# One ordered stretch of all engines from the mixer to the end, and the up weights of the second feed forward's first pair as events of their own

## The chip, the core and the metric

The kernel runs on one core of a Trainium2 chip. The metric is device time in microseconds (us) of one launch; lower is better. Engines are named as the profile names them: PE (matmuls), PEld (weight loads of PE), DVE, ACT, POOL, and SP, which here only issues DMAs.

## The reference, cut to what matters

One transformer layer on 512 tokens of width 1024, in float32: a feed forward at half weight, a token mixer, a second feed forward at half weight, and a last norm.

```python
x = x + 0.5 * swiglu(rmsnorm(x, ffn1_norm), w_gate1, w_up1, w_down1)
x = x + token_mixer(rmsnorm(x, mix_norm), w_in, w_out, ...)
x = x + 0.5 * swiglu(rmsnorm(x, ffn2_norm), w_gate2, w_up2, w_down2)
return rmsnorm(x, final_norm)

def swiglu(x, w_gate, w_up, w_down):
    return (jax.nn.silu(x @ w_gate) * (x @ w_up)) @ w_down
```

The change lies where the mixer's last product (`w_out`) passes into the second feed forward. That feed forward has 22 tiles of 128 hidden columns, each with a gate and an up product over 1024 inputs (eight steps `k` of 128).

## The kernel before, in words

**Three matmuls for one.** Every float32 operand is split into a high part and a rest (the low part), both in the format that PE multiplies fast. A product is then three matmuls: high by high, high by low, low by high (`mm3`, L143 to L146). The split costs two instructions for each weight block: a cast on ACT that makes the high part, then a subtraction on DVE that makes the low part from the raw block and the high part. So a weight is ready for PE when its DMA has landed, ACT has cast it and DVE has subtracted.

**Places.** Raw weights land in a ring of three buffers (tag `raw`, L130). High and low parts go into a ring of three places in `w_all` (`w_place`, L124 to L127). A new weight waits until PE has read the old one in its place, and a new raw block until DVE has read the old one in its buffer.

**The second feed forward** (`ffn`, L225) has two stages. `turned_front` (L914) makes tiles 0 and 1: it transposes the mixer's result into `xh`/`xl`, runs `first_mm` and `tile_mm` (gate and up of tiles 0 and 1), and prepares combinations of the normed input (`normed_t`, L279, four pairs `p`; tiles `nx`, `th`, `tl`, in the profile `nxb`, `txb`, `ttb`). `gated` (L1010) makes `silu(gate) * up` of a tile and splits it into `ah` and `al`. `pipeline` (L835) then does the up products of the tiles `n1` and `n1 + 1` (`up`, L303; `n1` is 2 here) over 16 steps of 0.68 us, and after them the block units: pairs of tiles by a scheme with seven products instead of eight (`SEVEN`, L46), each product with its own weight. The first unit is `("g", n1)`. Its products are called `a11`, `s3`, `s2`, `a12`, `s1`, `a22`, `s4` here, after the weight that each reads; its first one writes `pwgb` in the profile. The weights `s2` and `s4` are sums that DVE makes (`total`, L396); `s1` and `s3` are summed by a DMA that POOL issues (`weight_sums`, L364).

**What sets the order.** The tile framework lets the order of an engine's instructions be written by hand inside `tc.manual_schedule(engines=...)`. Inside one such stretch an engine takes its instructions as the program issues them. Two stretches that follow each other on the same engine are each kept in order, but a scheduler may weave the second into the end of the first. Before the change, this part of the kernel has three stretches for DVE and ACT: the mixer's (L1761), `turned_front`'s (L1083) and `pipeline`'s (L1085). PE has one stretch over the whole kernel (L90); SP and POOL have one over `turned_front` and `pipeline`. Within `turned_front` and `pipeline` the order comes from planned times: `ev(t, f, ...)` and `at(time, rank, f, ...)` collect calls with a time in us or ns, and the calls are made in the order of these times. The times fix an order and nothing else; on the chip an instruction starts when its engine and its inputs are ready.

**The up weights before the change.** `up_weights(j)` (L313) loads the up weight of tile `j`, casts it and splits it, in one call. For tile `n1` it is called inside `turned_front`, as an event at step 5 of the eight steps of `tile_mm` (L1073). For tile `n1 + 1` it is called first thing in `pipeline`, ahead of the loop over the up products (L877). The raw block is `raw_sub` in the profile, its high and low parts are places of `w`, and the product is `pub`.

**One small instruction** belongs to the stretches too: `wo_tail` (L1874), called from `turned_front`, doubles the gains of the second norm, `V.tensor_scalar_mul(sm[:, 2 * KD:3 * KD], ..., 2.0)`, 128 x 8 elements on DVE.

Of the kernel before, what the change touches and what calls it, by code (L numbers as in the profile page):

```python
# [84 lines left out]
def tile_macaron(ctx: ExitStack, tc, xs, xT, wf, wgu1, wst1, wd1, wdg1, wqk, wvw, wv, wo, wgu2, wst2,  # L85
# [38 lines left out]
    def w_place(shift=0):  # L124
        o = w_used[0] % 3 * 1024 + shift
        w_used[0] += 1
        return w_all[:, o:o + 1024], w_all[:, 3072 + o:4096 + o]  # L127

    def load_w(src, nm, n=1024, shift=0):
        raw = wp.tile([P, 1024], F32, tag="raw", name=f"raw_{nm}")  # L130
        nc.sync.dma_start(raw[:, :n], src)
        return (raw, *w_place(shift))
# [5 lines left out]
    def get_w(src, nm, n=1024, shift=0):  # L138
        raw, h, l = load_w(src, nm, n, shift)
        split_w(raw, h, l, 0, n)  # L140
        return h, l
# [83 lines left out]
    def ffn(wgu, wst, wd, wdg, n0, n1, norm, early, res, nm, hooks, ended, first=None,  # L225
# [77 lines left out]
        def up(j):  # L303

            wh, wl = up_w[j]
            pu = ups[j] = pp.tile([P, S], F32, tag="t", name=f"pu{nm}{j}", bufs=2)
            for k in range(KD):
                o = k // 2 * P + k % 2 * 4 * P
                o = slice(o, o + P)
                mm3(pu[:], wh[:, o], wl[:, o], xh[k][:], xl[k][:], k == 0, k == KD - 1)  # L310
                yield k

        def up_weights(j):  # L313
            up_w[j] = get_w(wst[j - n1][1], f"su{nm}{j}")

        ups, up_w, g = {}, {}, {}
# [31 lines left out]
        def sum_slots(u):  # L348
            if u[0] == "d":
                return GROUP_SUMS[u[2] // 2 % 2]  # L350
            if final is not None:
                if u == units[0]:
                    return TURNED_FIRST
                return GROUP_SUMS[(u[0] == "u") ^ (u[1] in TURNED_PAIRS[1])]
            if u == units[0]:
                return PAIR_SLOTS[0][:2]
            if u[1] == PLAIN + 8:
                return GROUP_SUMS[u[0] == "u"]
            o = 2 if u[0] == "g" else 4
            return PAIR_SLOTS[(u[1] - PLAIN) // 2 % 4][o:o + 2]  # L360
# [155 lines left out]
        def at(time, rank, f, *a):  # L516
            count[0] += 1
            heapq.heappush(events, (time, rank, count[0], f, a))
# [4 lines left out]
        def run(until):  # L523
            while events and events[0][0] <= until:
                _, _, _, f, a = heapq.heappop(events)
                f(*a)
# [308 lines left out]
        def pipeline():  # L835
            seen = {}
            for t, (u, o, p) in enumerate(ops):
                if o[0] == "p":
                    at(starts[t] - 2 * PLAIN_STEP, 1, load, u)
                    at(starts[t] - 3 * STEP, 3, high, t)  # L840
                    at(starts[t] - 2 * STEP, 2.5, low, t)
                elif u[0] == "t":
                    block_events(t)
                elif u[0] == "P":
                    at(starts[t] - (8 if p == 0 else 9) * STEP, 1.5, tiles_load, u, p)
                    at(starts[t] - (3 if p == 0 else 4) * STEP, 4.5, high, t)
                    at(starts[t] - (2 if p == 0 else 3) * STEP, 2.5, low, t)
                else:
                    if t == begin[u]:
                        if u != units[0]:  # L850

                            time, s0 = starts[t] - 14 * STEP, sum_slots(u)
                            if s0 in seen:
                                time = max(time, starts[begin[seen[s0]] + 2])
                            seen[s0] = u
                            if u == ("g", PLAIN + 10) and final is None:


                                time += STEP
                            if u == ("g", TURNED_PAIRS[1][0]) and final is not None:  # L860
                                time += 3 * STEP
                            at(time, 1, weight_sums, u)
                        if final is None:
                            at(starts[t] - 7 * STEP, 1.5, load, u)
                        else:
                            at(starts[t] - 7 * STEP, 1.5, load, u, (0,))
                            at(starts[t] - 5 * STEP, 2.2, load, u, (1,))
                    if o[0] in ("s2", "s4"):
                        at(starts[t] - 5 * STEP, 2, total, t)
                    at(starts[t] - 4 * STEP, 3, high, t)  # L870
                    at(starts[t] - 3 * STEP, 2.5, low, t)
                at(starts[t], 4, product, t)
            if bias is not None:
                at(starts[begin["p", plain]], 5, bias[0])
                for j in range(BIAS_STEPS):
                    at(starts[begin["d", 1, 0] + 2 + j], 5, bias[1], j)
            up_weights(n1 + 1)  # L877
            for i in range(2):
                for k in up(n1 + i):
                    prepared(n1 + i, k)  # L880
                    run((8 * i + k - 15) * 680)
            run(1 << 40)

        def block_events(t):
            u, o, p = ops[t]
            now = starts[t]
            if o[0] in TURNED_AHEAD:
                at(starts[begin[u]] - TURNED_AHEAD[o[0]][u[1]][p] * STEP, 2.2, block_load, u, o[0], p)
            elif o[0] in ("a12", "a22"):
                at(now - 8 * STEP, 1.5, block_load, u, o[0], p)  # L890
            if (u[1], o[0]) == (1, "s4"):
                now = starts[begin[u]] + (TURNED_KEPT[p] + 5) * STEP
            if o[0] in ("s2", "s4"):
                at(now - 5 * STEP, 2, total, t)
            at(now - 4 * STEP, 3, high, t)
            at(now - 3 * STEP, 2.5, low, t)
            if t == begin[u] and u[1] == 1:
                at(now + 2 * STEP, 1, final, "begin", now + 2 * STEP, put, None)
# [10 lines left out]
        def prepared(j, k):  # L909
            if (j, k) in prepare:  # L910
                f, p = prepare[j, k]
                f(p)

        def turned_front():  # L914

            todo = []
            now = [0.0]

            def ev(t, f, *a):
                todo.append((t, len(todo), f, a))  # L920

            def pe(cost, f, *a):
                ev(now[0], f, *a)
                now[0] += cost
# [108 lines left out]
            for hf in range(2):  # L1033
                ev(2.4 + 2.6 * hf, gate_load, hf)
                for c in range(2):
                    t = (7.0, 10.0)[hf] + 0.62 * c
                    ev(t, gate_high, hf, c)
                    ev(t + 0.7, gate_low, hf, c)
            for k in range(KD):
                t = (z[1] + 0.5 + 0.42 * k) if k < 4 else z[2] + 0.5 + 0.42 * (k - 4)  # L1040
# [5 lines left out]
            t0 = now[0]  # L1046
# [10 lines left out]
            for k in range(KD):  # L1057
                t = (t2 if k < 4 else max(t3, t2 + 1.7)) + 0.3 + 0.42 * (k % 4)
# [9 lines left out]
            gated(0, now[0] + 0.1)  # L1068
            for p, t in enumerate((0.2, 4.2, 8.0, 12.0)):
                ev(now[0] + t, normed_t, p)  # L1070
            for k in range(KD):
                if k == 5:
                    ev(now[0], up_weights, n1)  # L1073
                pe(1.36, tile_mm, k)
            gated(1, now[0] + 0.1)
            for _, _, f, a in sorted(todo, key=lambda e: (e[0], e[1])):
# [2 lines left out]
        order = ExitStack()  # L1079
        if final is not None:  # L1080
            prepare = {}
            order.enter_context(tc.manual_schedule(engines={mybir.EngineType.SP, mybir.EngineType.Pool}))
            with tc.manual_schedule(engines={mybir.EngineType.DVE, mybir.EngineType.Activation}):  # L1083
                turned_front()
            with order, tc.manual_schedule(engines={mybir.EngineType.DVE, mybir.EngineType.Activation}):  # L1085
                pipeline()
            return
        for j in range(j0, n1):
# [9 lines left out]
            for hf in range(2):  # L1098
                wh, wl = get_w(wgu[j, hf], f"gu{nm}{j}_{hf}")
                for kk in range(4):  # L1100
                    k = hf * 4 + kk
# [38 lines left out]
    with tc.manual_schedule(engines={mybir.EngineType.DVE, mybir.EngineType.Activation}):  # L1140
        for t in range(4):
            raw = wp.tile([P, 1024], F32, tag="raw", name=f"raw_f{t}")
            h, l = w_place()
            for kk in range(2):
                k = 2 * t + kk
# [74 lines left out]
    n1 = {}  # L1220
# [537 lines left out]
    load(2)  # L1758
    prep(0, True)
    prep(1, True)  # L1760
    with tc.manual_schedule(engines={mybir.EngineType.PE, mybir.EngineType.DVE,  # L1761
                                     mybir.EngineType.Activation}):
        lows = []
        for t in range(max(len(chunks), max(at) + 1)):
            evs = sorted(at.get(t, []), key=lambda e: e[0])
            for r, f, a in evs:
                if r < 10:
                    f(*a)
            if t < len(chunks):
                chunks[t]()  # L1770
            for r, f, a in evs:
                if r >= 10:
                    f(*a)
            for _ in range((t != held["hold"]) + (t - 1 == held["hold"])):
                if lows:
                    lows.pop(0)()
            if later:
                hi_, lo_ = later.pop(0)
                hi_()
                lows.append(lo_)  # L1780
        assert not later
        for f in lows:
            f()
# [277 lines left out]
```

## Time and profile before

| | us |
|---|---|
| median of 3 runs | 922.3 |
| lowest and highest of them | 922.28, 925.2 |
| the profiled execution, its own time | 922.4 |
| its span, first to last instruction | 920.6 |
| granted TensorE clock (share of full) | 0.999 |
| PE busy | 909.9 (99%) |
| DVE busy | 731.8 (79%) |
| ACT busy | 550.5 (60%) |
| POOL busy | 118.5 (13%) |

The profile is one execution. The span runs from the first to the last instruction; the execution's own time is 1.8 us longer. The shares are means over the whole span: DVE's 79% holds stretches that are nearly full and others that are not. A matmul's duration in the timeline is longer than its share of PE's time, because matmuls overlap; the distance from one start to the next is what counts. `L135` and `L136` are the lines of the cast and of the subtraction in the helper `split_w`, `L443` and `L447` those of the block units' weights; a helper's line stands for all who call it, so tiles are named beside lines.

### The profile page before, as it was taken

The numbers are of one execution on the slowest core, as the hardware profiler recorded it, in microseconds if no ns is written. First come the engines' busy times: TensorE is split into PE (matmuls) and PEld (weight loads), VectorE is DVE, ScalarE is ACT, GpSimd is POOL, SyncE is SP. The second block draws the span as 40 slices with busy tenths as digits, with TensorE's granted clock in tenths as the row PEclk, the third lists the DMA queues.
The fourth block names the chain that finished last, engine by engine and source line by source line (L and its number), as shares of the span: only waits on it lengthen the run. The fifth ranks groups of instructions, "written<-read, shape, count | busy, mean of one in ns | idle before, by whom it ended". The sixth has DMA issues, their size and how long they took to land.

```text
span 920.6 us, 16495 instructions
## 1 busy us (share of the span) xinstructions
PE 909.9 (99%) x6014; PEld 829.8 (90%) x6014; DVE 731.8 (79%) x1525; ACT 550.5 (60%) x1155; POOL 118.5 (13%) x157
## 2 busy tenths in 40 slices
PE   9999999999999999999999999999999999999997
PEld 7888999999999998888989778979999889999885
DVE  7797887686888897968876545887887887888786
ACT  7454665345665675656766676656666446666564
POOL 0001100112201100073000000011131012211100
PEclk9999999999999999999999999999999999999999
DMA  7456646578856563457443204375798369787722
GB/s 257 128 146 156 161 116 171 147 171 203 222 137 182 154 173 112 142 154 228 121 116 114 69 30 132 92 180 131 187 236 209 91 181 245 196 190 201 202 70 92
DMA packets 64593, 143.66 MB, mean 156 GB/s; under 512 B 7872, under 2 KB 8384, under 8 KB 64512
## 3 DMA queue, kind: packets, MB, share of 16 engines
q1 hardware_dynamic: 47856, 110.93, 37.3%
q0 software_dynamic: 16656, 31.68, 20.5%
q8 instruction: 47, 0.77, 0.3%
q14 instruction: 34, 0.28, 0.1%
HBM read 135.20 MB, written 4.24 MB: 151 GB/s over the span
## 4 chain that ended last, share of the span: by engine, by line
PE 92%; DVE 4%; DMA 2%; issue 1%; ACT 1%; SPq 0%; DVEq 0%; ACTq 0%
PE pt L145 3%; PE pt L144 3%; PE pt L146 3%; PE pwo L144 2%; PE pwo L146 2%; PE pwo L145 2%; PE pua L146 2%; PE pua L145 2%; PE pua L144 2%; PE pq L144 2%; PE pq L146 1%; PE pq L145 1%; PE pk L144 1%; PE pk L146 1%; PE pk L145 1%; PE pda L146 1%
## 5 line engine op out<-in xcount | busy, mean ns | idle before, releaser
L1508 ACT ACTIVATE pr<-pr,mx 128x128 f32<-128x128 f32 (+3 forms) x64 | 36.1, 565 | 37.4 <-DVE mx L1505 37.3
L1505 DVE CUSTOM_DVE_ANT_0 pr<-sc,strip 128x128 f32<-128x128 f32 (+3 forms) x64 | 30.6, 488 | 19.4 <-PE sc L1503 19.1
L372 POOL DMA_DIRECT2D s1bg<-wst_dram x10 | 8.7, 868 | 271.8 <-DVE fin L1889 160.5
L443 ACT CAST w<-s2a 128x512 fp32r<-128x512 f32 x46 | 28.6, 622 | 15.0 <-DVE s2a L406 12.1
L447 DVE TENSOR_TENSOR w<-s2a,w 128x512 fp32r<-128x512 f32 x46 | 31.6, 686 | 6.5 <-ACT w L443 6.5
L447 DVE TENSOR_TENSOR w<-s2b,w 128x512 fp32r<-128x512 f32 x38 | 26.1, 687 | 9.4 <-ACT w L443 9.4
L1714 POOL DMA_DIRECT2D xn_rows<-xt x32 | 20.6, 655 | 64.1 <-DVE xt L1711 64.1
L443 ACT CAST w<-s2b 128x512 fp32r<-128x512 f32 x38 | 23.6, 620 | 6.3 <-DVE s2b L406 5.5
L144 PE MATMUL pq<-xh,w 128*128 128x512 f32 x64 | 26.7, 417 | 0.0
L144 PE MATMUL pwo<-w,mh 128*128 128x512 f32 x64 | 25.9, 404 | 0.0
L146 PE MATMUL pq<-xh,w 128*128 128x512 f32 x64 | 25.1, 392 | 0.0
L145 PE MATMUL pq<-xl,w 128*128 128x512 f32 x64 | 25.1, 392 | 0.0
L144 PE MATMUL pk<-xh,w 128*128 128x512 f32 x64 | 25.1, 392 | 0.0
L145 PE MATMUL pwo<-w,mh 128*128 128x512 f32 x64 | 25.0, 391 | 0.0
L146 PE MATMUL pk<-xh,w 128*128 128x512 f32 x64 | 25.0, 391 | 0.0
L146 PE MATMUL pwo<-w,ml 128*128 128x512 f32 x64 | 25.0, 391 | 0.0
L145 PE MATMUL pk<-xl,w 128*128 128x512 f32 x64 | 24.9, 390 | 0.0
L1312 DVE TENSOR_TENSOR w<-raw_qk,w 128x512 fp32r<-128x512 f32 x28 | 19.0, 688 | 4.6 <-ACT w L1308 4.5
L145 PE MATMUL pwgb<-xl,w 128*128 128x256 f32 x80 | 22.5, 281 | 0.0
L145 PE MATMUL pxgb<-ttb,w 128*128 128x256 f32 x80 | 22.5, 281 | 0.0
L146 PE MATMUL pwgb<-xh,w 128*128 128x256 f32 x80 | 22.5, 281 | 0.0
L144 PE MATMUL pwgb<-xh,w 128*128 128x256 f32 x80 | 22.5, 281 | 0.0
(712 smaller groups left out, 3946.3 us busy)
## 6 DMA issues: line engine op xcount, KB each, us to landing
raw_qk<-wqk_dram SPq DMA_DIRECT2D x16, 512.0 KB, 3.5
raw0bg<-wst_dram SPq DMA_DIRECT2D x10, 512.0 KB, 5.5
raw0bu<-wst_dram SPq DMA_DIRECT2D x9, 512.0 KB, 6.1
raw_gua<-wgu_dram SPq DMA_DIRECT2D x8, 512.0 KB, 3.4
raw0ag<-wst_dram SPq DMA_DIRECT2D x8, 512.0 KB, 5.1
raw0ad<-wdg_dram SPq DMA_DIRECT2D x8, 512.0 KB, 4.4
strip<-bias_rows SPq DMA_DIRECT2D x16, 256.0 KB, 3.8
raw_wo<-wo_dram SPq DMA_DIRECT2D x8, 512.0 KB, 3.4
```

Source lines behind the costliest of these rows:

```text
L144: T.matmul(po, wh, mh, start=first, stop=False, skip_group_check=on)
L145: T.matmul(po, wh, ml, start=False, stop=False, skip_group_check=on)
L146: T.matmul(po, wl, mh, start=False, stop=last, skip_group_check=on)
L372: nc.gpsimd.dma_start(t[:], b, accum_op=ALU.add)
L443: A.copy(made[t][0], source(t))
L447: V.tensor_tensor(l, source(t), h.bitcast(F32), op=ALU.subtract)
L1312: V.tensor_tensor(l[:, c:c + 512], raw[:, c:c + 512], h[:, c:c + 512].bitcast(F32), op=ALU.subtract)
L1505: V.tensor_tensor_reduce(out=pi, in0=ps[:, :w], in1=st["b"][m][:, w - 1::-1], op0=ALU.add, op1=ALU.min, scale=1.0, scalar=3.0e38, accum_ou ...
L1508: A.activation(pi, pi, AF.Exp, scale=-1.0, bias=st["mx"][:, m, i:i + 1], accum_out=st["ls"][:, m, i:i + 1])
L1714: nc.gpsimd.dma_start(bass.AP(tensor=ap.tensor, offset=ap.offset + m * P + a * NB, ap=[[D, NB], [NB * D, S // NB], [1, NB]]), t[a * NB:(a ...
```

## The change

The diff has three parts.

1. `up_weights(n1)` and `up_weights(n1 + 1)` are taken apart. Load, cast and subtraction become events of `turned_front`: the loads at `t0 + 12` and `t0 + 16`, where `t0` is the planned start of `first_mm`; the casts at 2.6 and 8.4 us after the planned start of `tile_mm`, and the subtractions 1.3 us after each cast. `pipeline` skips its own call.
2. `turned_front` and `pipeline` lose their stretches for DVE and ACT. The one for SP and POOL stays.
3. The mixer's stretch for PE, DVE and ACT is entered on the kernel's exit stack and is left only at the end. So DVE and ACT take all their instructions from the mixer on exactly as the program issues them.

```diff
@@ pipeline
-            up_weights(n1 + 1)
+            if n1 + 1 not in up_w:
+                up_weights(n1 + 1)
@@ turned_front
             for p, t in enumerate((0.2, 4.2, 8.0, 12.0)):
                 ev(now[0] + t, normed_t, p)
+            raw_up = {}
+
+            def up_load(j):
+                raw_up[j], *up_w[j] = load_w(wst[j - n1][1], f"su{nm}{j}")
+
+            def up_high(j):
+                cast(up_w[j][0], raw_up[j][:])
+
+            def up_low(j):
+                rest(up_w[j][1], raw_up[j][:], up_w[j][0])
+
+            for i, t in enumerate((2.6, 8.4)):
+                ev(t0 + 12 + 4 * i, up_load, n1 + i)
+                ev(now[0] + t, up_high, n1 + i)
+                ev(now[0] + t + 1.3, up_low, n1 + i)
             for k in range(KD):
-                if k == 5:
-                    ev(now[0], up_weights, n1)
                 pe(1.36, tile_mm, k)
@@ ffn
-            order.enter_context(tc.manual_schedule(engines={mybir.EngineType.SP, mybir.EngineType.Pool}))
-            with tc.manual_schedule(engines={mybir.EngineType.DVE, mybir.EngineType.Activation}):
+            with tc.manual_schedule(engines={mybir.EngineType.SP, mybir.EngineType.Pool}):
                 turned_front()
-            with order, tc.manual_schedule(engines={mybir.EngineType.DVE, mybir.EngineType.Activation}):
                 pipeline()
@@ the mixer
-    with tc.manual_schedule(engines={mybir.EngineType.PE, mybir.EngineType.DVE,
-                                     mybir.EngineType.Activation}):
+    ordered = ctx.enter_context(ExitStack())
+    ordered.enter_context(tc.manual_schedule(engines={mybir.EngineType.PE, mybir.EngineType.DVE,
+                                                      mybir.EngineType.Activation}))
+    if True:
```

## The prediction

> **What bounds the kernel now.** I read the page of the profile first, then the list of PE's waits, because one row of the page already names the bound.
>
> ```profile
> span 920.6 us, 16495 instructions
> PE 909.9 (99%) x6014; PEld 829.8 (90%) x6014; DVE 731.8 (79%) x1525; ACT 550.5 (60%) x1155; POOL 118.5 (13%) x157
> ```
>
> PE is busy for 99% of the span, so only what makes PE stand still, or lets it run on, can move the end. The view of waits, kept to PE, is short enough to show whole (engine, line, what it waited for: us in total, times, longest):
>
> ```profile
> PE pub L146 <- DVE w L136: 1.4, 1, 1.4
> PE warm L1131 <- POOL ones_d L1125: 1.0, 1, 1.0
> PE pga L1176 <- ACT w L1156: 0.8, 1, 0.8
> PE pub L144 <- ACT w L135: 0.7, 1, 0.7
> PE sc L1503 <- DMA l<-l: 0.2, 1, 0.2
> ```
>
> Two of the five are on `pub`, the product that reads the up weights that the change moves. The windows around it show that this is the only place in the middle of the kernel where PE stops (columns: stretch, length, busy time of PE, PEld, DVE, ACT, POOL, granted clock, DMA share, GB/s):
>
> ```profile
> 593.00:604.10 11.10, 11.10 (x51) 9.01 (x50) 10.13 (x21) 6.09 (x9) 1.19 (x2) 1.00 0.47 149
> 604.10:607.10 3.00, 0.95 (x4) 0.36 (x3) 2.55 (x4) 1.36 (x3) 0.53 (x1) 1.00 0.93 191
> 607.10:617.64 10.54, 10.54 (x46) 8.68 (x47) 9.74 (x22) 6.09 (x13) 1.72 (x2) 1.00 0.66 146
> ```
>
> PE is solid in the first and third stretch and has 0.95 us of work in the 3.00 us between. Note the DVE column too: 10.13 of 11.10 and 9.74 of 10.54. DVE is nearly full on both sides of the gap, so what the gap gives DVE is not free. PE's timeline prices the gap (start, duration, what, idle before it and who ended it):
>
> ```profile
> 603.86 0.39 PE L146 MATMUL pub<-xh,w 128*128 128x512 f32 x1
> 604.95 0.50 PE L144 MATMUL pub<-xh,w 128*128 128x512 f32 x1 [0.70 <-ACT w L135]
> 605.29 0.40 PE L145 MATMUL pub<-xl,w 128*128 128x512 f32 x1
> 607.03 0.50 PE L146 MATMUL pub<-xh,w 128*128 128x512 f32 x1 [1.35 <-DVE w L136]
> 607.38 0.40 PE L144 MATMUL pub<-xh,w 128*128 128x512 f32 x1
> 617.18 0.39 PE L145 MATMUL pub<-xl,w 128*128 128x512 f32 x1
> 617.64 0.28 PE L144 MATMUL pwgb<-xh,w 128*128 128x256 f32 x1
> 617.88 0.28 PE L146 MATMUL pwgb<-xh,w 128*128 128x256 f32 x1
> ```
>
> Undisturbed, 512-wide matmuls start 0.227 us apart and 256-wide ones 0.12. The 48 matmuls of the two `up` products follow the one at 603.86, so the first `pwgb` could start at 603.86 + 49 x 0.227 = 614.97. It starts at 617.64. **The gap and the slow restart behind it cost 2.67 us**, of which about 0.2 is the restart (607.03 to 607.38 is 0.35, not 0.23, and the next few are 0.01 slow).
>
> Why were the weights late? ACT and DVE in the same stretch:
>
> ```profile
> 598.67 1.05 ACT L135 CAST w<-raw_sub 128x1024 fp32r<-128x1024 f32 x1 [0.71 <-PE pub L145]
> 599.62 0.62 ACT L927 CAST ahb<-t1b 128x512 fp32r<-128x512 f32 x1
> 603.86 1.04 ACT L135 CAST w<-raw_sub 128x1024 fp32r<-128x1024 f32 x1
> 598.59 0.69 DVE L1017 TENSOR_TENSOR t1b<-pub,t1b 128x512 f32<-128x512 f32 x1
> 599.75 1.23 DVE L136 TENSOR_TENSOR w<-raw_sub,w 128x1024 fp32r<-128x1024 f32 x1 [0.47 <-ACT w L135]
> 604.55 0.69 DVE L406 TENSOR_TENSOR s2b<-s1bg,raw0bg 128x512 f32<-128x512 f32 x1 [0.66 <-DMA raw0bg<-wst_dram]
> 605.16 0.69 DVE L295 TENSOR_TENSOR ttb<-nxb,txb 128x512 fp32r<-128x512 f32 x1
> 605.76 1.22 DVE L136 TENSOR_TENSOR w<-raw_sub,w 128x1024 fp32r<-128x1024 f32 x1
> ```
>
> There are two up weights. In the order of instructions of the old program the cast at 598.67 waits for PE to free a place: it belongs to the second tile (n1+1, needed last), and the one at 603.86 to the first. The two ordered stretches were woven the wrong way round. DVE also meets a sum of the next unit, which waits 0.66 us for a DMA, ahead of the first tile's low half.
>
> **The change part by part.** The order of instructions of the changed program has the same instructions on every engine, and the same order on PE, SP and POOL. Only DVE and ACT differ, in two places.
>
> *The doubling of the norm's gains* moves from the start of the kernel to the output projection.
>
> ```profile
> 4.62 0.17 DVE L1077 TENSOR_SCALAR x<-x 128x8 f32<-128x8 f32 x1
> ```
>
> At the start PE's only DVE-side neighbour, `pga`, waits for ACT in the list above, not for DVE, so taking 0.17 us off DVE gains nothing. At its new place, between splits of `raw_wo`, the list has no PE wait either. Its bounds are 0.17 us either way; I take 0.
>
> *The up weights and everything behind them.* New order on ACT: `ah` of tile 0, cast n1, two `txb` casts of pair 1, two of pair 2, cast n1+1, `silu` of tile 1, four casts of pair 3, `ah` of tile 1, then the first weights of the block units. DVE follows suit. The sum and splits of the first block unit (`g`, n1), formerly woven in from 604.55 on, now all stand behind `al` of tile 1. The durations, from the groups of this stretch and two timeline rows:
>
> ```profile
> L295 DVE TENSOR_TENSOR ttb<-nxb,txb 128x512 fp32r<-128x512 f32 x6 | 4.1, 688 | 0.2
> L294 ACT CAST txb<-nxb 128x512 fp32r<-128x512 f32 x6 | 3.7, 624 | 5.6 <-DVE nxb L286 4.2 <-DVE nxb L289 1.4
> L299 ACT CAST ttb<-nxb 128x256 fp32r<-128x256 f32 x4 | 1.5, 403 | 0.8 <-DVE nxb L289 0.8
> 601.49 0.42 DVE L285 TENSOR_TENSOR nxb<-nxb 128x256 f32<-128x256 f32 x1
> 601.95 0.42 DVE L286 TENSOR_TENSOR nxb<-nxb,nxb 128x256 f32<-128x256 f32 x1
> ```
>
> A 0.69 us DVE operation lets the next start after 0.60 (605.16 to 605.76); a dependent one starts 0.04 after the end (601.49 to 601.95 is 0.46), and so does a hand-over between engines. From `t1b` at 598.59, which does not move:
> - ACT: `ah` 599.32 to 599.94, cast n1 599.85 to 600.90. DVE: `al` 599.98, low half n1 600.94 to 602.17. PE wants the high half at 604.09 and the low at 604.54. **Both come 2.4 us or more early: the gap at 604 goes**, if the load is there:
>
> ```profile
> 580.85 10.74 SPq L131 DMA_DIRECT2D raw_sub<-wst_dram  x2
> DMA to landing us min/median/max: 3.4/4.0/4.6
> ```
>
> The loads keep their place in SP's queue; the second is issued near 591.3 and lands before 596.
> - DVE, pairs 1 and 2: each takes four `nxb` (4 x 0.46), a wait for the second cast, and two `ttb`, 3.12 us in all: 602.08 to 608.32. Cast n1+1 runs 607.59 to 608.64 on ACT, its low half 608.68 to 609.91 on DVE. PE wants it at 604.09 + 26 x 0.227 = 609.98. That is 0.03 us of room after the hand-over: level.
> - DVE then: `t1b` of tile 1 609.82, four `nxb` from 610.42, four half `ttb` 612.15 to 613.56, `al` 613.56, the sum 614.16, and the low half of `a11`, the first block weight, 614.76 to 615.45. ACT has its high half by 614.05.
> - PE reaches `pwgb` at 614.97 and wants that low half two matmuls later, at 615.21. It comes at 615.49. **A new wait of 0.28 us, PE on DVE.** Behind it every later split gains room (`s3`'s low half 616.05 against 616.9, `s2`'s 616.65 against 618.3), so this wait is the last.
>
> The sum: the third `pwgb` matmul moves from 617.88 to 615.49, a gain of 2.39 us. No restart after so short a stop is in the trace; its cost lies between 0 and the 0.2 after the long one; I take 0.15, nearer to the only row there is. **Gain 2.24 us**, from both sides: 2.67 if DVE is never late, 1.8 if each of eleven hand-overs takes 0.04 more. Nothing behind 618 has a PE wait to absorb or return it. DVE's new standing order delays one load, the raw block of the second unit, which waits for a buffer:
>
> ```profile
> 607.01 0.33 SPq L380 DMA_DIRECT2D raw0bg<-wst_dram  x1
> DMA to landing us min/median/max: 4.9/5.5/9.5
> ```
>
> It follows the second up weight's low half, so 609.95 instead of 607.01; SP's raw and sum loads behind it follow. Even at 9.5 us it lands at 619.5, and PE starts that unit at 625.4: covered. If it were not, each us late would be a us lost.
>
> The profiled execution took 922.4 us with a span of 920.6; 922.4 - 2.2 = 920.2. The median of the runs is 0.1 lower: **920.1 us**, span 918.4.
>
> One rule speaks against packing DVE. A DMA issue of POOL beside it:
>
> ```profile
> 601.30 0.86 POOL L372 DMA_DIRECT2D s1bg<-wst_dram  x1 [16.20 <-DMA s3bg<-wst_dram]
> ```
>
> Both DVE rows at 601.49 and 601.95 lie inside it and last their usual 0.42, so nothing is held up here. The Trainium skill, page "SBUF — State Buffer", section "Who interferes with whom", says that DVE and GpSimd share one port pair as an exclusive lock, for DVE's two-port modes and some two-input operations, and that the later one blocks fully. By that rule the dense DVE stretch would pay for each POOL issue; the two rows above don't bear it out.
>
> **The rivals.**
> - *A: DVE keeps up.* For it: 0.03 and -0.28 us are within the reading error of a chain of twenty steps. The gap goes whole: -2.67, 919.6 us.
> - *B: DVE becomes the bound for longer.* For it: the windows' 10.13 of 11.10. Hand-overs and conflicts cost 1 us more along the chain: gain 1.2, 921.1 us. Against: pitches in the rows repeat to 0.01.
> - *C: POOL's issues hold DVE.* Four fall between 601 and 611, 0.86 us each. If each stops DVE for its length, `a11`'s low half is ready 3.4 us later, at 618.9 instead of 617.88 before: +1.0 and the restart, 923.5 us, slower than before. It decides from 2.4 us of blocking on. Against: 0.42 us inside the POOL row.
> - *D: the change doesn't do what it says.* Excluded for the order, which the changed program shows; left is that something outside the chain moves.
>
> **How the numbers follow.** Forecast 0.68 (919.8 to 920.8); A 0.14; B 0.10; C 0.04; D 0.04, either way. 0.3%, about what a measurement can tell from no change, is 2.8 us: faster means below 919.5, slower above 925.1. The forecast and B lie within. Of A about half falls below 919.5 by scatter, 0.07, and with tails and D 0.12 faster. Slower by that much needs C and more: 0.03. Same 0.85. The range, 919.4 to 921.5, takes in the forecast, A and the better half of B.
>
> **What would show it.** Both PE waits on L135 and L136 at `pub` gone; the low half of n1 done by 602.2; `pwgb` starting near 615.0; one PE wait of about 0.3 us there, on DVE's L447; all else as before. A PE wait on `pub` for the second tile, or on `pwgb` above 0.8 us, is B; DVE operations stretched beside POOL's rows, C; a PE wait for `raw0bg` behind 625 would make the prediction wrong altogether.

## The result, and the profile after

| | us |
|---|---|
| before, median of 12 runs (lowest to highest) | 922.24 (921.72 to 925.2) |
| after, median of 12 runs (lowest to highest) | 920.07 (919.28 to 922.39) |
| ratio after to before | 0.9974, 95% interval 0.9964 to 0.9983 |
| after, the profiled execution and its span | 920.74, 919.0 |

The kernel is 2.2 us faster, 1.6 to 3.3 by the interval; 2.24 was forecast. At 0.26% the result falls just short of the 0.3% that the forecast took as what can be told from no change; the interval, 0.17 to 0.36%, lies on both sides of that bound and wholly on the faster side.

PE's list of waits after the change, whole:

```profile
PE warm L1143 <- POOL ones_d L1137: 1.0, 1, 1.0
PE sc L1515 <- DMA l<-l: 0.4, 1, 0.4
PE pga L1188 <- ACT w L1168: 0.3, 1, 0.3
```

Both rows on `pub` are gone, and no row has come for them. The windows of before, asked of the trace after:

```profile
593.00:604.10 11.10, 11.10 (x55) 9.36 (x54) 9.90 (x20) 5.04 (x7) 1.72 (x2) 1.00 0.45 148
604.10:607.10 3.00, 3.00 (x15) 2.49 (x14) 2.81 (x7) 1.15 (x3) 0.00 (x0) 1.00 1.04 223
607.10:617.64 10.54, 10.54 (x53) 8.75 (x53) 10.06 (x20) 7.58 (x15) 1.74 (x2) 1.00 0.68 155
```

In the middle one PE is now busy for 3.00 us of 3.00 where it was 0.95. DVE, third of the busy columns, is a little fuller than it was, 2.81 for 2.55 and 10.06 for 9.74 in the last two: the stop went, the load of DVE stayed.

This profiled execution cannot be laid over the one of before by its clock time, because it is 0.8 us late long before the change. Its first `pua` and `pga` matmuls show most of it (rows of after, then of before):

```profile
5.62 0.63 PE L1188 MATMUL pua<-eha,w 128*128 128x512 f32 x1
6.05 0.63 PE L1188 MATMUL pga<-eha,w 128*128 128x512 f32 x1
```

```profile
5.62 0.39 PE L1176 MATMUL pua<-eha,w 128*128 128x512 f32 x1
5.86 0.40 PE L1176 MATMUL pga<-eha,w 128*128 128x512 f32 x1
```

The matmuls start 0.43 us apart instead of 0.24, until 6.9 us in the one execution, from 5.6 us on not in the other. In e2 below, matmuls behind a stop start 0.42 to 0.43 us apart at a granted clock of 0.52, so half the clock is the likely reason; it is not shown, since the clock column reads 1.00 for both starts. The change is not the reason: e5, the same kernel, has 0.23 from 5.81 us on, and e1, with the start of before, has 0.43 until 6.20. So times inside the stretch are counted from DVE's product `t1b<-pub` of tile 0, which the change leaves where it was: 598.59 before, 599.38 after.

### The profile page after: what moved, and what is told of

Read it like the earlier page. It is cut to its first block, busy times and chain, and to the rows that moved or that the text cites. A ratio compares the mean times of both kernels' runs of the same rounds, so it can differ in the third digit from the quotient of the medians.

```text
span 919.0 us, 16498 instructions
## 1 busy us (share of the span) xinstructions
PE 910.7 (99%) x6014; PEld 830.8 (90%) x6014; DVE 731.8 (80%) x1525; ACT 549.6 (60%) x1155; POOL 118.2 (13%) x157
## 4 chain that ended last, share of the span: by engine, by line
PE 94%; DVE 3%; DMA 1%; ACT 1%; issue 1%; DVEq 0%; SPq 0%; ACTq 0%
PE pt L146 3%; PE pt L145 3%; PE pt L144 3%; PE pwo L144 2%; PE pwo L145 2%; PE pwo L146 2%; PE pua L144 2%; PE pua L145 2%; PE pua L146 2%; PE pq L144 2%; PE pq L146 1%; PE pq L145 1%; PE pk L144 1%; PE pk L146 1%; PE pk L145 1%; PE pda L146 1%
```

## The experiments

**The theory**, called the order theory in the expectations: two operations for each of two weights stood behind work that waits for late things; put ahead of it, they let PE run on until DVE's chain stops it, by a quarter of a us. **Rivals**: one ordered stretch is enough without the events (stretch theory); the events are enough without the stretch (events theory); only the doubling that left the start counts (start theory); and the forecast's A and B, on how near DVE is to being the bound.

One number of each trace tells them apart better than the median does, since the start and the rest of the run stay out of it: the distance from `t1b` of tile 0 on DVE to the third `pwgb` matmul on PE, the first that needs a block weight's low half. "Chain expected" is worked out from the forecast: 16.90 with its short stop, 16.62 without it, and on top of that the waits or differences that each kernel's expectation gives.

| kernel | distance, us | chain expected | median, us | before, same chip | ratio, 95% interval |
|---|---|---|---|---|---|
| before | 19.29 | | 922.24 | | |
| the change | 16.78 | 16.90 | 920.07 | 922.24 | 0.9974 (0.9964 to 0.9983) |
| e5 the change again | 16.78 | 16.90 | 919.90 | 921.99 | 0.9979 (0.9969 to 0.9989) |
| e1 events only | 19.21 | 19.60 | 923.61 | 922.39 | 1.0013 (1.0004 to 1.0023) |
| e2 stretch only | 21.97 | 20.92 | 925.06 | 922.39 | 1.0034 (1.0021 to 1.0046) |
| e3 two more on DVE | 18.23 | 18.10 | 921.43 | 922.39 | 0.9995 (0.9986 to 1.0004) |
| e4 late split, one tile | 16.62 | 16.62 | 919.61 | 922.39 | 0.9973 (0.9964 to 0.9982) |
| e6 late split, both | 16.63 | 16.62 | 919.92 | 921.99 | 0.9976 (0.9967 to 0.9985) |
| e7 gains first | 16.78 | 16.90 | 919.94 | 921.99 | 0.9977 (0.9968 to 0.9986) |
| e8 first up weight late | 17.54 | 17.42 | 920.68 | 921.99 | 0.9988 (0.9979 to 0.9996) |
| e9 three more on DVE | 18.97 | 18.70 | 922.39 | 921.72 | 1.0009 (0.9993 to 1.0024) |
| e10 four more on DVE | 19.70 | 19.30 | 924.13 | 921.72 | 1.0022 (1.0010 to 1.0034) |

### e1: the events without the stretch

```diff
-            with tc.manual_schedule(engines={mybir.EngineType.SP, mybir.EngineType.Pool}):
+            order.enter_context(tc.manual_schedule(engines={mybir.EngineType.SP, mybir.EngineType.Pool}))
+            with tc.manual_schedule(engines={mybir.EngineType.DVE, mybir.EngineType.Activation}):
                 turned_front()
+            with order, tc.manual_schedule(engines={mybir.EngineType.DVE, mybir.EngineType.Activation}):
                 pipeline()
@@ the mixer
-    ordered = ctx.enter_context(ExitStack())
-    ordered.enter_context(tc.manual_schedule(engines={mybir.EngineType.PE, mybir.EngineType.DVE,
-                                                      mybir.EngineType.Activation}))
-    if True:
+    with tc.manual_schedule(engines={mybir.EngineType.PE, mybir.EngineType.DVE,
+                                     mybir.EngineType.Activation}):
```

> Only the events of the up weights, with the three stretches of before. In its order of instructions the first block unit's sum, cast and split of raw0bg are again woven into the front, now ahead of the second up weight, and the gains are doubled at the start again. Theory (order theory): the gain of the change needs every split that waits for something late to stand behind the up weights; here DVE meets the sum that waits for raw0bg near 603 and ACT the cast of raw0bg near 601.5, both wait until it has landed near 604.5 to 605.3, and the second up weight's high half comes near 610.6 to 611 on the scale of before instead of 608.6. PE waits some 2 us at the second up product, for ACT, and 0.8 more for DVE's low half. Time 922.8 us, 0.6 above before, 2.7 above the change. Rival (events theory): the events alone take the gap away, about 920.1. Rival (start theory): only the doubling that left the start matters; then this one, which has it at the start, stays at 922.2.

923.61 us; the gain is gone and a little more. ACT, DVE and PE in its timeline:

```profile
603.86 0.62 ACT L443 CAST w<-raw0bg 128x512 fp32r<-128x512 f32 x1 [3.18 <-DMA raw0bg<-wst_dram]
603.85 0.69 DVE L406 TENSOR_TENSOR s2b<-s1bg,raw0bg 128x512 f32<-128x512 f32 x1 [1.12 <-DMA raw0bg<-wst_dram]
609.89 1.04 ACT L928 CAST w<-raw_sub 128x1024 fp32r<-128x1024 f32 x1
610.99 0.50 PE L144 MATMUL pub<-xh,w 128*128 128x512 f32 x1 [1.50 <-ACT w L928]
612.25 0.50 PE L146 MATMUL pub<-xh,w 128*128 128x512 f32 x1 [0.53 <-DVE w L931]
```

The first up weight comes early, as with the change. But the block unit's first weight is woven in ahead of the second one, and ACT stands 3.18 us and DVE 1.12 us at the head of their queues for a DMA whose data nobody needs yet. The second cast comes at 609.89, and PE waits where the chain had it wait. Events and start theories had 920.1 and 922.2: the events alone are not enough. In the median it is 0.8 us slower than expected, while its trace is 0.4 quicker; its runs scatter from 921.4 to 926.1. Each run's mean granted clock sorts them: five of the eleven have 0.996 or 0.997 and took 923.4 to 923.9; of the six with 0.998 or 0.999, four took 921.4 to 922.4, the profiled one among them, and two 924.1 and 926.1. So a fall of the clock behind the two stops, as e2 shows one next, is the likelier reason for the 0.8 us. No trace shows such a run, so this is argued, and for the two longest at full clock no reason is known; a late landing of `raw0bg` could be one.

### e2: the stretch without the events

```diff
-            raw_up = {}
...
-            for i, t in enumerate((2.6, 8.4)):
-                ev(t0 + 12 + 4 * i, up_load, n1 + i)
-                ev(now[0] + t, up_high, n1 + i)
-                ev(now[0] + t + 1.3, up_low, n1 + i)
             for k in range(KD):
+                if k == 5:
+                    ev(now[0], up_weights, n1)
                 pe(1.36, tile_mm, k)
```

> Only the one ordered stretch; the up weights are loaded, cast and split in one call each, where they were before. Order theory: the first up weight is cast behind pair 1 of the normed input, the second only behind the last split of tile 1. From the durations of before: the first one's low half is done near 605.3 instead of 604.5 wanted, a wait of 0.8 us; the second one's cast starts when tile 1 is split, near 611.9, so PE waits 2.7 us for it and 0.8 for the low half. pwgb starts 4.0 us later than in the change: 924.1 us, 1.9 above before. Rival (stretch theory): one ordered stretch is what helps, 920.1 to 921. Start theory: the doubling stands late here too, so 920.1.

925.06 us: slower than before, as the order theory had it, and 1 us slower than it had it. PE in the timeline, and the window behind the second stop (the last columns are granted clock, DMA share, GB/s):

```profile
605.27 0.50 PE L146 MATMUL pub<-xh,w 128*128 128x512 f32 x1 [0.52 <-DVE w L136]
610.16 0.39 PE L146 MATMUL pub<-xh,w 128*128 128x512 f32 x1
612.88 0.72 PE L144 MATMUL pub<-xh,w 128*128 128x512 f32 x1 [2.33 <-ACT w L135]
613.39 0.63 PE L145 MATMUL pub<-xl,w 128*128 128x512 f32 x1
```

```profile
612.88:616.00 3.12, 3.00 (x6) 1.92 (x7) 3.12 (x5) 2.12 (x4) 0.96 (x2) 0.52 0.61 93
```

The two stops lie where the chain put them, at 605.3 and 612.9. What it lacked stands in the clock column: 0.52 for 3.1 us behind the stop of 2.33. PE started six matmuls there. About ten would have fitted at full clock, by an estimate from e1's spacings behind its stops, 0.34 us and then 0.23, with the low half ready at 614.09 as here; the slow spacing goes on to 616.43. That is the missing 1.05 us (21.97 against 20.92). All five runs of e2 have a mean clock of 0.996 or 0.997. e9 and e10 ask whether the stop's length did it.

### e3, e9, e10: more work on DVE ahead of the block units

```diff
                 def low_():
-                    rest(al[j][:], gs[j][:], ah[j][:])
+                    for _ in range(1 + 2 * j):
+                        rest(al[j][:], gs[j][:], ah[j][:])
```

> The change, with the last split on DVE ahead of the block units (al of tile 1) made three times instead of once: two more operations of 0.69 us, 0.60 apart, same result. If DVE sets the start of the block units, as the forecast has it, PE waits 1.2 us longer there and nothing gives it back: 921.3 us, 1.2 above the change. Rival A (DVE keeps up and has room): the first 0.6 or more is hidden, at most 0.6 above the change, 920.1 to 920.7.

PE's wait in e3:

```profile
PE pwgb L146 <- DVE w L447: 1.4, 1, 1.4
```

921.43 us, 1.4 above the change; the distance grows by 1.45, where 1.20 was expected. No part of it is hidden: DVE sets the start of the block units, and A's room of 0.6 doesn't exist. That it is more is a matter of size, seen below in e10's row. With 3 and 4 in place of the 2:

> The change with the last split of tile 1 made four times instead of once, same result: PE stands still for about 2.0 us at the third pwgb matmul (1.42 us were measured with two more, and each adds 0.60). Clock theory: the stop of 2.33 us that cost 1.05 us more than its length lost it to the halved clock behind it; a stop of 2.0 us may lie under or over the point from which the clock falls. Under it: 1.8 us above the change, 921.8. Over it: 1.0 to 1.4 more, 923.0, with a granted clock near 0.5 for some 3 us behind the stop. Rival (chance: the clock fell there for a reason of its own): no fall here, 921.8.

> The same made five times: a stop of 2.6 us. Clock theory: longer than 2.33 us, so the clock falls in most executions: 2.4 us for the stop and 1.0 to 1.4 for the clock, 923.4 to 923.8, with a granted clock near 0.5 behind it. Rival (chance): 2.4 us above the change, 922.4, full clock.

The third `pwgb` matmul of e9 and the one after it, and a window of e9:

```profile
617.45 0.39 PE L146 MATMUL pwgb<-xh,w 128*128 128x256 f32 x1 [2.15 <-DVE w L447]
617.67 0.28 PE L144 MATMUL pwgb<-xh,w 128*128 128x256 f32 x1
```

```profile
617.00:620.00 3.00, 2.55 (x21) 2.55 (x22) 3.00 (x6) 2.34 (x5) 0.00 (x0) 1.00 0.01 3
```

The same of e10, with two matmuls a little later:

```profile
614.71 0.28 PE L145 MATMUL pwgb<-xl,w 128*128 128x256 f32 x1
617.88 0.39 PE L146 MATMUL pwgb<-xh,w 128*128 128x256 f32 x1 [2.89 <-DVE w L447]
619.31 0.41 PE L145 MATMUL pzgb<-ttb,w 128*128 128x256 f32 x1
619.52 0.42 PE L146 MATMUL pzgb<-txb,w 128*128 128x256 f32 x1
```

```profile
617.88:619.16 1.28, 1.28 (x11) 1.28 (x11) 1.28 (x3) 1.28 (x4) 0.00 (x0) 1.00 0.00 0
619.16:622.20 3.04, 3.04 (x17) 3.04 (x16) 2.27 (x4) 0.92 (x4) 0.00 (x0) 0.51 0.21 61
```

After e9's idle 2.15 us the clock column stays at 1.00. After e10's 2.89 PE runs 1.3 us at full clock and then drops to 0.51, with 0.21 us between starts where 0.12 is usual, for some 3.3 us until 622.5. So e2's fall was no chance: a stop of this length can bring it. The medians agree: e10 lies 2.4 us above its before, e9 0.7, with an interval that takes in no difference. Both are above what was expected: e9's 922.39 lies between the 921.8 of a kept clock and the 923.0 of a fallen one, e10's 924.13 beyond 923.4 to 923.8. The mean clocks of the runs suggest why for e9: it is 0.996 or 0.997 in three of its ten, the three longest, 923.4 to 926.7. In e10 it is 0.995 to 0.997 in seven of ten. So 2.15 us of idle time may bring the fall too, only less often; this is argued from the means, which do not say where in a run the clock fell. The third and fourth operation cost 0.74 and 0.73 us of distance, not 0.60. DVE's row of e10 says why:

```profile
613.02 3.60 DVE L931 TENSOR_TENSOR alb<-t1b,ahb 128x512 fp32r<-128x512 f32 x5
```

Five operations in 3.60 us are 0.73 from start to start: each writes the tile of the one before, and so starts 0.04 behind its end, as dependent operations do, where independent ones overlap.

### e4 and e6: DVE relieved

e4 moves cast and split of tile 1 behind the first weights of the block units, e6 of both tiles:

```diff
                 ev(t, silu)
                 ev(t + 0.7, up_)
+                if j == 1:
+                    kept_back.extend((high_, low_))
+                    return
                 ev(t + 1.5, high_)
                 ev(t + 2.2, low_)
@@ pipeline
+            for i, f in enumerate(kept_back):
+                at(starts[2 + i], 6, f)
```

> The change, with cast and split of tile 1 (ah, al) moved behind the seven first weights of the block units, where both engines have room; they are needed much later. If DVE is the bound at pwgb by 0.14 to 0.3 us, the short stop there goes and no more: 919.8 to 919.95 us, 0.1 to 0.3 below the change, with no stop at the third pwgb matmul in the trace. If DVE were the bound by much more (rival B), up to 0.6 below. If it isn't the bound, no difference.

> The change, with cast and split of both tiles 0 and 1 moved behind the first weights of the block units. That takes two DVE operations of 0.69 us out of the stretch ahead of pwgb. Order theory: PE is the bound as soon as one of them is out, since moving tile 1's alone took the stop away, so the second brings nothing: 919.6 to 919.9 us, as with one. Rival (DVE still the bound somewhere ahead): 0.6 less than with one, 919.0.

Third `pwgb` matmul and its forerunner in e4, then in e6:

```profile
615.09 0.28 PE L145 MATMUL pwgb<-xl,w 128*128 128x256 f32 x1
615.20 0.28 PE L146 MATMUL pwgb<-xh,w 128*128 128x256 f32 x1
```

```profile
614.36 0.28 PE L145 MATMUL pwgb<-xl,w 128*128 128x256 f32 x1
614.48 0.28 PE L146 MATMUL pwgb<-xh,w 128*128 128x256 f32 x1
```

The spacing is 0.12 in both: the stop is gone with one split moved, and the second brings 0.00 more (16.62, 16.63). PE is the bound from there. In the medians 0.16 us can't be seen; e4's 919.61 and e6's 919.92 don't differ from the change by what these runs can tell.

### e7: the doubling back at the start

```diff
                     V.tensor_scalar_mul(early[0][0][:], x[0], gain(0, 0))
+                    V.tensor_scalar_mul(sm[:, 2 * KD:3 * KD], sm[:, 2 * KD:3 * KD], 2.0)
...
-        ev(-1, V.tensor_scalar_mul, sm[:, 2 * KD:3 * KD], sm[:, 2 * KD:3 * KD], 2.0)
```

> The change, with the doubling of the gains put back to the kernel's start, behind the first high part of x. Order theory: DVE has room there, PE waits for ACT and for the first weights, so no difference: 920.1 us, within 0.3. Rival (start theory): the 0.17 us operation lies on the way to the first low part and comes back whole at the end, 920.3 or more, with PE waiting on DVE in the first ten us.

919.94 us beside 919.90 for the change on the same chip, and PE's list of waits has no row on DVE in the start. The move is worth nothing that shows.

### e8: the first up weight late

```diff
-                ev(now[0] + t, up_high, n1 + i)
-                ev(now[0] + t + 1.3, up_low, n1 + i)
+                if i:
+                    ev(now[0] + t, up_high, n1 + i)
+                    ev(now[0] + t + 1.3, up_low, n1 + i)
             for k in range(KD):
+                if k == 5:
+                    ev(now[0], up_high, n1)
+                    ev(now[0], up_low, n1)
```

> The change, with only the first up weight's cast and split back at step 5 of tile_mm, behind pair 1; the second stays where the change has it. Order theory: the first low half is done near 605.3 on the scale of before instead of the 604.54 wanted; PE waits 0.8 us there. DVE's chain behind it is as long as in the change, so the short stop at pwgb goes in exchange: 0.5 to 0.7 us above the change, 920.6 to 920.8. The second up weight then owns most of the 5 us that the ordered stretch without the events costs. Rival (a stop costs its whole length wherever it lies): 0.9 to 1.0 above, 921.0.

```profile
604.92 0.50 PE L146 MATMUL pub<-xh,w 128*128 128x512 f32 x1 [0.52 <-DVE w L931]
615.65 0.28 PE L145 MATMUL pwgb<-xl,w 128*128 128x256 f32 x1
615.76 0.28 PE L146 MATMUL pwgb<-xh,w 128*128 128x256 f32 x1
```

920.68 us, 0.78 above the change: between the 0.5 to 0.7 of the order theory and the 0.9 to 1.0 of its rival, so the median cannot decide. The distance can. One stop has come, 604.92, and the one at `pwgb` has gone (0.11 between the two). The new stop costs 17.54 - 16.62 = 0.92 us, of which the 0.16 of the old one goes off: 0.76 us, and not its whole length. Of the 5.2 us between e2 and the change the first up weight owns 0.8; the rest is the second one's stop and the clock behind it.

## Why the prediction was right, point by point

Rows of the trace after that carry the chain; ACT, DVE, PE and SP:

```profile
600.62 1.04 ACT L928 CAST w<-raw_sub 128x1024 fp32r<-128x1024 f32 x1
601.70 1.23 DVE L931 TENSOR_TENSOR w<-raw_sub,w 128x1024 fp32r<-128x1024 f32 x1 [0.26 <-ACT w L928]
608.30 1.04 ACT L928 CAST w<-raw_sub 128x1024 fp32r<-128x1024 f32 x1
609.37 1.23 DVE L931 TENSOR_TENSOR w<-raw_sub,w 128x1024 fp32r<-128x1024 f32 x1 [0.25 <-ACT w L928]
615.42 0.68 DVE L447 TENSOR_TENSOR w<-raw0bg,w 128x512 fp32r<-128x512 f32 x1
604.65 0.39 PE L146 MATMUL pub<-xh,w 128*128 128x512 f32 x1
610.77 0.40 PE L146 MATMUL pub<-xh,w 128*128 128x512 f32 x1
615.78 0.28 PE L144 MATMUL pwgb<-xh,w 128*128 128x256 f32 x1
615.90 0.28 PE L145 MATMUL pwgb<-xl,w 128*128 128x256 f32 x1
616.16 0.39 PE L146 MATMUL pwgb<-xh,w 128*128 128x256 f32 x1
616.38 0.28 PE L144 MATMUL pwgb<-xh,w 128*128 128x256 f32 x1
610.62 0.33 SPq L380 DMA_DIRECT2D raw0bg<-wst_dram  x1
```

- **The gap at `pub` goes.** From the last `tile_mm` matmul at 604.65 to the first `pwgb` at 615.78 are 11.13 us for 49 steps, 0.227 each: nothing between them. The first low half is ready at 602.93, 3.55 us after `t1b`; 3.58 was reckoned.
- **The second up weight is level.** Its low half is ready at 610.60 and PE takes it at 610.77: 0.17 us of room, 0.13 after a hand-over of 0.04, where 0.03 was reckoned. A step later in DVE's order, and PE would have stopped here too.
- **A new short wait at `pwgb`.** 615.90 to 616.16 is 0.26, not 0.12: 0.14 us, half of the 0.28 forecast, and too short for a row in the list of waits. The low half of `a11` ends 16.72 us after `t1b`; 16.86 was reckoned. e3 shows that DVE's chain sets this moment, e4 that the stop goes when the chain is shorter.
- **The restart.** 616.16 to 616.38 is 0.22, and 0.12 behind it: 0.10 where 0.15 was taken.
- **The sum.** The distance shrinks by 19.29 - 16.78 = 2.51 us, 2.39 forecast; with the restart 2.41 against 2.24, and 2.2 in the medians. The mechanism came as forecast, but that 920.1 met 920.07 to 0.03 us is luck: the distance was missed by 0.12, and the medians of before alone lie between 921.72 and 922.39.
- **Costed at nothing.** The doubling: e7, 0.0. The raw block of the second unit is issued 11.24 us after `t1b`, 11.36 reckoned, and PE never waits for it.
- **The rivals.** A, DVE keeps up, is e4's order and not the change's: the difference is 0.16 us. B is out: the chain was a little shorter than reckoned. C, DVE held by POOL's issues, isn't borne out after the change either: a DVE operation inside a POOL issue lasts as long as ever. The prediction read the rule more widely than it stands: the Trainium skill's "SBUF — State Buffer", section "Who interferes with whom", says that a DVE operation with two inputs in SBUF contends with a GpSimd instruction that reads SBUF, and not with one that only writes it. No run here shows whether a DMA issue of POOL reads SBUF, so these rows do not go against that section.

```profile
603.29 0.43 DVE L286 TENSOR_TENSOR nxb<-nxb,nxb 128x256 f32<-128x256 f32 x1
602.97 0.86 POOL L372 DMA_DIRECT2D s3bg<-wst_dram  x1
```

- **The range and the chances** held. The change's median stays 0.6 us short of the bound of 0.3%, about what medians of before differ by from one set of runs to the next.

The prediction's *reason* for the gain was two orders in one, and e1 and e2 part them: the events without the stretch lose the gain because DMA waits come to the head of two queues, the stretch without the events loses the gain and 2.7 us more, because the second up weight then waits for everything else and the clock falls behind that stop.

## What to carry to other kernels

Where one engine is 99% busy, write out what it waits for, and follow the two or three instructions behind that wait through their engines' queues by durations and hand-overs from the trace; here that gave the outcome of a re-ordering to 0.2 us, by the trace's own distance. In an in-order queue ask of each instruction not only when it is needed but what it waits for: one that stands for a DMA too early holds up all that follow. And when a stop of the bounding engine is taken away, look at once for the engine that had used the pause: the gain ends where that one's chain begins.

## What the runs showed of the hardware that was not expected

A stop of PE can cost more than its length. Counted from the start of the last matmul to the start of the next, PE stood for 2.43 us in e9 and kept its clock in the profiled execution; it stood 2.72 us in e2 and 3.17 us in e10 and then ran at 0.51 to 0.52 of it for some 3.3 us, in e10 only after 1.3 us at full clock. That cost e2 1.05 us on top of the stop. The Trainium skill, "TensorE: Matmul & The Clock Gate", section "Part 1: The HAM clock gate", gives about 3.4 us for the idle window after which the clock is halved, and says that the window runs freely; here 2.72 us from start to start, 2.33 of them idle, was enough, and the measurement decides.

It is a matter of odds and not of one bound, as far as each run's mean clock tells. The mean is 0.997 or less in five of five runs of e2, seven of ten of e10, five of eleven of e1 (two stops close together, 1.50 and 0.53 us idle), three of ten of e9, and eight of 79 of before (0.70 and 1.35 us idle); the profiled executions of e2 and e10, whose fall the traces show, have 0.996 and 0.997. It is 0.998 or 0.999 in all 78 runs of the change, e3, e4, e5, e6, e7 and e8, where the longest stop in this stretch is the 1.42 us of e3. So in about a tenth of its runs before seems to lose some clock that the change saves. The mean does not say where in a run the clock was lost, and six of the eight come from one of three chips, so this is argued, not shown.

A place that the change doesn't touch has no room left in some executions: in e4 and e9, one `pygb` product between 779 and 790 us waited 0.4 us for ACT, in the other profiles not. In e4 ACT had stood 1.74 and 1.55 us for `raw0bg` and `s3bg` just before, in e9 0.94 and 2.46, in the trace after 1.56 and 0.53. The late loads alone do not explain it: in e3 ACT stood 2.45 us for `s3bg` there, and PE did not wait. The cause is open.

```profile
772.11 0.62 ACT L443 CAST w<-s3bg 128x512 fp32r<-128x512 f32 x1 [1.55 <-DMA s3bg<-wst_dram]
779.56 0.39 PE L144 MATMUL pygb<-txb,w 128*128 128x256 f32 x1 [0.40 <-ACT pygb L526]
```
